# Layer 1's memory attention at the start of the layer instead of at its end

## The chip, the cores and the metric

The kernel runs on one core of one Trainium2 chip, and the metric is the device time of one execution in microseconds. The engines meant below are PE (the matrix engine; PEld is its loading of weights), ACT (the scalar engine), DVE (the vector engine), POOL, and SP, which here issues the loads of the weights. Each engine works through its own instructions in a fixed order. PSUM is the small memory that PE writes its results to, in banks of 128 x 512 fp32.

## The reference, cut to what matters

One inference step of a decoder of two layers runs over 256 prompt tokens and 8 decode sequences of one token, 264 columns in all, with 2048 features. Layer 0 mixes tokens by windowed attention, layer 1 by a gated linear recurrence (HGRN2) with 12 heads of 128. Each layer has besides 4 memory heads, which attend to 256 memory rows: for the prompt these are projected from `mem_prompt`, for each decode sequence they come from a cache of its own. The 12 recurrence heads and the 4 memory heads make 16 blocks of 128 features, which are gated and projected:

```
mq, g, q, f, iv = split(h @ w_in)
fg = lb + (1 - lb) * sigmoid(f)                 # decay, per head and token
state[t] = fg[t] * state[t-1] + (1 - fg[t]) outer iv[t]
o = silu(q)[t] @ state[t];  o = o * rsqrt(mean(o*o) + eps) * norm_w
mem = softmax(mq @ mk.T / sqrt(128)) @ mv       # mk, mv: projected, or cached
y = concat(o, mem) * silu(g) @ w_out
h = layer_norm(alpha * h + y) * ln_w + ln_b
```

## The kernel before, in words

All activations lie transposed, features on the 128 partitions and the 264 columns along the row. The weights come as tiles of 128 x 2048 fp32 (1 MB), one for each block of 128 output features. A class `Stream` (from L50) takes them in one fixed list of *units*: SP loads a tile into one of 4 raw buffers (L77), ACT rounds it to fp16 into one of 4 split buffers (`hl`, L92), DVE takes the remainder (L93), and then the unit's function runs. A projection (`proj`) is 48 matmuls of 264 columns: 16 blocks of the contraction, each in three passes, weights' high half by the data's high half (L297), by its low half (L298), and weights' low half by the data's high half (L299). It goes to one of two PSUM banks ("pj"), from which the next engine reads it. Cache tiles and recurrence states come through the same stream; a cache tile is used by 64 matmuls of one or two columns (mss, L646/L647, for key scores; mso, L690/L691, for sums of values), a state tile (half as large) by 17 (hos).

Longer work that hangs on several units is written as *side* generators: `hg_side(pi)` for a pair of heads of the recurrence, `memp_side` for the prompt's memory attention, the layer norm. After each unit `pump(1)` advances them by a step, and `drain()` finishes them. `hg_side` goes through the levels 1 to 64 of a tree over the prompt's blocks (products hs on PE, then copies and products on DVE and ACT), then builds the head outputs (hpo, L1079 to L1081), reads them to `osb` (ACT L1083), squares them (L1087), sums the squares over partitions by a matmul (rms, L1092), takes the reciprocal root by a Ln (L1093) and an Exp (L1095) on ACT, each with a load of its function table (ACT_TABLE_LOAD) before it, and scales (DVE L1098). For heads 8 to 11 the result is multiplied by the gate later, in `gate_by`: DVE L722, ACT L723 (the fp16 high half, in `bhl`), DVE L724 (the low half). The 16 output projections (`out_unit`) contract over these 16 blocks in order, c = 0 to 15, so that block c = 10 and 11 of every output need heads 10 and 11.

The order of layer 1's units before: memory keys and values; for each pair of heads f, f, v, v, then q, state and (heads 0 to 7) gate g of each head; then the four memory queries mq, the prompt's four memory sides tied to the last of them; then key cache tiles ck0 to ck3 and value cache tiles cv0 to cv3 with the late gates g8 to g13 behind the first six of them, and g14, g15 at the end; then the outputs. The compiler's scheduler takes the program in this order and fixes, from its own timing model, the order of the instructions on each engine; it may place a unit's small pieces in the midst of another's matmuls. Names in the rows below: g113 is gate 13 of layer 1, o10 and o11 are its outputs 0 and 1, hl151 is the split tile of unit 151 of the stream; hpo5, rms50 and rms51 belong to the last pair, heads 10 and 11. PSUM tags are pj (2 banks), pt (2), pv (1), ms (1) and sc (2).

Of the kernel before, what the change touches and what calls it, by code (L numbers as in the profile page):

```python
# [129 lines left out]
def trunk_kernel(  # L130
# [37 lines left out]

    def bank(tag, bufs, name):
        return ps.tile([P, 512], F32, tag=tag, name=name, bufs=bufs)  # L170

    stream = Stream(nc, cp, 4, 4)

# [379 lines left out]
        nc.scalar.activation(mix[:, :NQ, TP:T], pov, AF.Copy, scale=1.0 / (SA * SP))  # L553
        done[0].add("swa")

    def mq_unit(h):
        def fn(hl):
            pt = proj(hl, xhl, T, f"mq{h}")
            split_from(mqhl[:, 0, h], mqhl[:, 1, h], pt, 1.0 / SW)

        return fn
# [72 lines left out]
    def ck_unit(l, t):  # L634
        def fn(hl):
            v = hl.rearrange("p s (b h m) -> p s b h m", b=2, h=NM)
            if t == 0:
                mst["s"] = bank("ms", 1, f"mss{l}")
            sv = mst["s"][:, :128].rearrange("p (m r s) -> p m r s", m=2, s=2)
            for bb in range(2):  # L640
                b = 2 * t + bb
                for h in range(NM):
                    for m in range(2):
                        r = b * NM + h
                        ms = slice(m * P, (m + 1) * P)
                        mm(sv[:, m, r], v[:, 0, bb, h, ms], mqhl[:, :, h, TP + b], start=True, stop=False)  # L646
                        mm(sv[:, m, r, 0:1], v[:, 1, bb, h, ms], mqhl[:, 0, h, TP + b : TP + b + 1], start=False, stop=True)  # L647
            if t == 3:
                mems_soft(l)

        return fn
# [24 lines left out]
    def cv_unit(l, t):  # L676
        def fn(hl):
            v = hl.rearrange("p s (b m f) -> p s b m f", b=2, m=2)
            R = TS * NM
            phl = mst["p"].rearrange("p (m r) s -> p m r s", m=2)  # L680
            if t == 0:
                mst["o"] = bank("ms", 1, f"mso{l}")
            ov = mst["o"][:, :64].rearrange("p (h b s) -> p h b s", h=NM, s=2)
            for bb in range(2):
                b = 2 * t + bb
                for h in range(NM):
                    r = b * NM + h
                    f = slice(h * P, (h + 1) * P)
                    for m in range(2):
                        mm(ov[:, h, b], v[:, 0, bb, m, f], phl[:, m, r], start=m == 0, stop=False)  # L690
                        mm(ov[:, h, b, 0:1], v[:, 1, bb, m, f], phl[:, m, r, 0:1], start=False, stop=m == 1)  # L691
            if t == 3:
                so = cp.tile([P, NM, TS], F32, tag="mso", name=f"msos{l}")
                nc.vector.tensor_reduce(so, ov, axis=AX.X, op=ALU.add)
                nc.scalar.activation(mix[:, NQ:, TP:T], so, AF.Copy, scale=1.0 / (SA * SP))
                done[l].add("mem")

        return fn
# [174 lines left out]
        stream.add(wb(w_mk[1], h), mk_unit(1, h))  # L873
    for t in range(4):
        stream.add(wb(w_mv[1], t), mv_unit(1, t))

    l1 = ExitStack()
    H = {}
# [13 lines left out]
    def f_unit(h):  # L892
        def fn(hl):
            if h == 0:
                drain()
                open_l1()
            p1 = H["p"]
            pt = proj(hl, xhl, T, f"f{h}")
            i = h % 2
            if i == 0:  # L900
                cur["fg"] = p1.tile([P, 2, T], F32, tag="fg", name=f"fg{h}", bufs=2)
                cur["kk"] = p1.tile([P, 2, T], F32, tag="kk", name=f"kk{h}", bufs=2)
                cur["ks8"] = p1.tile([P, 2, TS], F32, tag="ks8", name=f"ks8{h}", bufs=2)
            fg, kk, ks8 = cur["fg"][:, i], cur["kk"][:, i], cur["ks8"][:, i]
            th = p1.tile([P, T], F32, tag="th", name=f"th{h}", bufs=2)
            nc.scalar.activation(th, pt, AF.Tanh, scale=0.5 * CP)
            half, mid, half_k, nhalf_k = (hl_lb[:, k, h : h + 1] for k in range(4))
            nc.scalar.activation(fg, th, AF.Identity, bias=mid, scale=half)
            nc.scalar.activation(kk, th, AF.Identity, bias=half_k, scale=nhalf_k)
            nc.vector.tensor_scalar_mul(ks8, kk[:, TP:T], 1.0 / (SA * SK))  # L910

        return fn
# [193 lines left out]
    def state_unit(h):  # L1106
        def fn(hl):
            p1 = H["p"]
            pi, i = h // 2, h % 2
            raw = stream.raw[state_at[h]][:, : TS * P]  # L1110
            R = raw.rearrange("p (b v) -> p b v", b=TS)
            v = hl[:, :, : TS * P].rearrange("p s (b v) -> p s b v", b=TS)
            vr, fgs, ks8 = cur["vr"][:, i], cur["fg"][:, i, TP:T], cur["ks8"][:, i]
            qs, ks, vts = (cur[n][:, i, TP:T] for n in ("q", "kk", "vt"))
            if i == 0:
                osb[pi] = p1.tile([P, 2, T], F32, tag="osb", name=f"osb{pi}", bufs=2)
            qk = p1.tile([P, TS], F32, tag="qk", name=f"qk{h}", bufs=2)
            qf = p1.tile([P, TS], F32, tag="qf", name=f"qf{h}", bufs=2)
            qfh = p1.tile([P, TS, 2], F16, tag="qfh", name=f"qfh{h}", bufs=2)
            nc.vector.scalar_tensor_tensor(qf, qs, SA * 0.5 * CP, fgs, op0=ALU.mult, op1=ALU.mult)  # L1120
            nc.vector.scalar_tensor_tensor(qk, qs, P * 0.5 * CP / SK, ks, op0=ALU.mult, op1=ALU.mult)
            nc.scalar.activation(qfh[:, :, 0], qf, AF.Copy)
            nc.vector.tensor_tensor(qfh[:, :, 1], qf, qfh[:, :, 0], op=ALU.subtract)
            po = bank("ms", 1, f"hos{h}")
            pov = po[:, : 2 * TS].rearrange("p (b s) -> p b s", s=2)
            for b in range(TS):
                mm(pov[:, b], v[:, 0, b], qfh[:, b], start=True, stop=False)
                mm(pov[:, b, 0:1], v[:, 1, b], qfh[:, b, 0:1], start=False, stop=True)
            pq = po[:, 2 * TS : 3 * TS]
            mm(pq, ones_rms, qk, start=True, stop=True)  # L1130
            nc.vector.tensor_reduce(qf, pov, axis=AX.X, op=ALU.add)
            nc.vector.tensor_tensor(qk, pq, vts, op=ALU.mult)
            nc.vector.scalar_tensor_tensor(osb[pi][:, i, TP:T], qf, 1.0 / (SA * SA), qk, op0=ALU.mult, op1=ALU.add)
            for g in range(2):
                pvb = bank("pt", 2, f"vb{h}{g}")
                for bb in range(4):
                    mm(pvb[:, bb * P : (bb + 1) * P], H["sel"][:, 4 * g + bb], vr, start=True, stop=True)
                for bb in range(4):
                    b = 4 * g + bb
                    s = R[:, b]  # L1140
                    nc.scalar.activation(s, s, AF.Copy, scale=fgs[:, b : b + 1])
                    nc.vector.scalar_tensor_tensor(
                        s, pvb[:, bb * P : (bb + 1) * P], ks8[:, b : b + 1], s, op0=ALU.mult, op1=ALU.add
                    )
            nc.gpsimd.dma_start(ss_o[pi, :, i * TS * P : (i + 1) * TS * P], raw)
# [4 lines left out]
    for pi in range(HD // 2):  # L1150
        for part, unit in (("f", f_unit), ("v", hv_unit)):
            for i in range(2):
                stream.add(wb(w_in1, NB1[part] + 2 * pi + i), unit(2 * pi + i))
        for h in (2 * pi, 2 * pi + 1):
            stream.add(wb(w_in1, NB1["q"] + h), hq_unit(h))
            state_at[h] = len(stream.units)
            stream.add(state[pi][:, (h % 2) * TS * P : (h % 2 + 1) * TS * P], state_unit(h), SA, whole=True)
            if h < NG1:
                stream.add(wb(w_in1, NB1["g"] + h), early_gate(h))
    for h in range(NM):  # L1160
        stream.add(wb(w_in1, NB1["mq"] + h), mq_unit(h))

    def mem1_sides(fn):
        return with_side(fn, [lambda h=h: memp_side(1, h) for h in range(NM)])

    u = stream.units[-1]
    stream.units[-1] = (u[0], mem1_sides(u[1]), *u[2:])

    def g1(j):
        stream.add(wb(w_in1, NB1["g"] + j), gate_unit(1, j))  # L1170

    late = deque(range(NG1, NC))
    for n, (c, unit, t) in enumerate([(c_mk, ck_unit, t) for t in range(4)] + [(c_mv, cv_unit, t) for t in range(4)]):
        stream.add(c[1, t], unit(1, t), SA)
        if late and (late[0] < NQ or n == 7 or late[0] < NQ + 2 and n > 3):
            g1(late.popleft())
    while late:
        g1(late.popleft())
    for i in range(NC):
        stream.add(wb(w_o[1], i), out_unit(1, i))  # L1180

    def after(i):
# [5 lines left out]
        if 1 <= i < 3:  # L1188
            spread_bias(2 * i - 2)
            spread_bias(2 * i - 1)  # L1190
        pump(1)
        for rows in due:
            rows()
        due[:], later[:] = later, []
# [141 lines left out]
```

## Time and profile before

| what | value |
|---|---|
| median of 3 runs | 912.54 us (911.29 to 913.2) |
| the profiled execution | 912.57 us, span 910.8 us |
| busy: PE, PEld, DVE, ACT, POOL | 895.5, 760.7, 701.9, 577.0, 34.6 us |
| mean granted clock of PE | 0.995 |
| from HBM | 179.80 MB read, 216 GB/s over the span with what is written |

The span runs from the first to the last instruction; the time of the execution holds a little more around it. Busy time of PE is the sum over its matmuls. In a table by stretches of time, the columns are the stretch, its length, the busy time of PE, PEld, DVE, ACT and POOL (with the number of instructions), then the granted clock of PE as a share of full speed, the busy share of the DMA engines and GB/s.

### The profile page before, as it was taken

Reading aid. Unit: us, or ns where it says so; the run is one execution under the profiler, and the core shown is the slowest. Engines: PE = TensorE matmul, PEld = TensorE weight load, DVE = VectorE, ACT = ScalarE, POOL = GpSimd, SP = SyncE. Lnnn points to the kernel's source line nnn. Section 1 sums busy time; section 2 is a strip of 40 time slices with the busy share of each in tenths; the row PEclk is TensorE's granted clock in tenths of the full one; section 3 lists DMA queues with packets and bytes.
Section 4 is the critical chain, followed back from the end, with each engine's and each line's share of the span. In section 5 each row is a group of like instructions: output and inputs, shape, how many; then the busy total and the mean of one; then the engine's idle time right before and its main releaser. Section 6 shows DMA issues by size and latency. Waiting matters only on the chain.

```text
span 910.8 us, 21139 instructions
## 1 busy us (share of the span) xinstructions
PE 895.5 (98%) x8913; PEld 760.7 (84%) x8913; DVE 701.9 (77%) x1280; ACT 577.0 (63%) x980; POOL 34.6 (4%) x63
## 2 busy tenths in 40 slices
PE   9999999999999999999999999999999999899996
PEld 6888989678888888866888888888888888788885
DVE  6869877669886666696697897978789899767645
ACT  6757776567664543576766777676778676945323
POOL 1100010000000000002000000000000000000000
PEclk9999999999999999999999999999999999999998
DMA  9999566567685555555384555727454778566302
GB/s 345 383 335 330 189 244 217 194 210 259 257 320 189 204 208 187 191 203 195 127 308 146 196 183 185 282 100 268 150 212 165 264 270 318 186 226 230 141 1 96
DMA packets 36412, 198.41 MB, mean 218 GB/s; under 512 B 4572, under 2 KB 8445, under 8 KB 16093
## 3 DMA queue, kind: packets, MB, share of 16 engines
q1 hardware_dynamic: 31632, 181.55, 55.6%
q0 software_dynamic: 4640, 15.44, 4.6%
q8 instruction: 70, 1.15, 0.5%
q14 instruction: 26, 0.21, 0.1%
q10 hardware_dynamic: 44, 0.07, 0.0%
HBM read 179.80 MB, written 17.22 MB: 216 GB/s over the span
## 4 chain that ended last, share of the span: by engine, by line
PE 87%; ACT 5%; DVE 5%; DMA 2%; issue 1%; SPq 0%; ACTq 0%; DVEq 0%
PE o L297 6%; PE o L299 6%; PE o L298 6%; PE g L299 6%; PE g L297 6%; PE g L298 6%; PE q L297 2%; PE hv L298 2%; PE hv L297 2%; PE q L298 2%; PE q L299 2%; PE hv L299 2%; ACT hl L92 2%; PE f L299 2%; PE f L297 2%; PE f L298 2%
## 5 line engine op out<-in xcount | busy, mean ns | idle before, releaser
L93 DVE SCALAR_TENSOR_TENSOR hl<-raw,hl 128x2048 f16<-128x2048 f32 (+2 forms) x176 | 376.9, 2145 | 96.6 <-ACT hl L92 95.9
L92 ACT ACTIVATE hl<-raw 128x2048 f16<-128x2048 f32 (+2 forms) x176 | 314.2, 1790 | 118.1 <-PE o L299 73.9
L297 PEld LDWEIGHTS <-hl 128*128 128x128 f16 (+1 forms) x2176 | 209.9, 98 | 34.0 <-issue 2.9
L299 PEld LDWEIGHTS <-hl 128*128 128x128 f16 (+1 forms) x2176 | 209.9, 98 | 33.4 <-DVE hl L93 2.1
L298 PEld LDWEIGHTS <-hl 128*128 128x128 f16 (+1 forms) x2176 | 209.9, 98 | 32.1 <-issue 1.6
L299 PE MATMUL g<-xhl,hl 128*128 128x264 f16 x512 | 141.3, 276 | 1.5 <-DVE hl L93 1.5
L297 PE MATMUL g<-xhl,hl 128*128 128x264 f16 x512 | 141.5, 276 | 0.0
L298 PE MATMUL g<-xhl,hl 128*128 128x264 f16 x512 | 141.3, 276 | 0.0
L299 PE MATMUL o<-mix,hl 128*128 128x264 f16 x512 | 141.2, 276 | 0.0
L298 PE MATMUL o<-mix,hl 128*128 128x264 f16 x512 | 141.2, 276 | 0.0
L297 PE MATMUL o<-mix,hl 128*128 128x264 f16 x512 | 140.8, 276 | 0.3 <-DVE xres L742 0.3
L297 PE MATMUL q<-xhl,hl 128*128 128x264 f16 x192 | 53.0, 276 | 1.0 <-DVE kst L245 1.0
L297 PE MATMUL f<-xhl,hl 128*128 128x264 f16 x192 | 52.9, 276 | 0.4 <-DVE mvhl L245 0.4
L297 PE MATMUL hq<-xhl,hl 128*128 128x264 f16 x192 | 53.0, 276 | 0.0
L298 PE MATMUL hq<-xhl,hl 128*128 128x264 f16 x192 | 53.0, 276 | 0.0
L299 PE MATMUL hq<-xhl,hl 128*128 128x264 f16 x192 | 53.0, 276 | 0.0
L298 PE MATMUL hv<-xhl,hl 128*128 128x264 f16 x192 | 53.0, 276 | 0.0
L297 PE MATMUL hv<-xhl,hl 128*128 128x264 f16 x192 | 53.0, 276 | 0.0
L299 PE MATMUL hv<-xhl,hl 128*128 128x264 f16 x192 | 53.0, 276 | 0.0
L298 PE MATMUL q<-xhl,hl 128*128 128x264 f16 x192 | 53.0, 276 | 0.0
L299 PE MATMUL q<-xhl,hl 128*128 128x264 f16 x192 | 53.0, 276 | 0.0
L299 PE MATMUL f<-xhl,hl 128*128 128x264 f16 x192 | 52.9, 276 | 0.0
(311 smaller groups left out, 1625.4 us busy)
## 6 DMA issues: line engine op xcount, KB each, us to landing
raw<-in_w_in SPq DMA_DIRECT2D x88, 1024.0 KB, 5.8
raw<-in_w_o SPq DMA_DIRECT2D x32, 1024.0 KB, 4.9
raw<-in_w_mk SPq DMA_DIRECT2D x8, 1024.0 KB, 4.8
raw<-in_w_mv SPq DMA_DIRECT2D x8, 1024.0 KB, 5.1
raw<-in_c_mk SPq DMA_DIRECT2D x8, 1024.0 KB, 5.2
raw<-in_c_mv SPq DMA_DIRECT2D x8, 1024.0 KB, 4.9
raw<-in_state SPq DMA_DIRECT2D x12, 512.0 KB, 5.0
out_ss<-raw POOLq DMA_DIRECT2D x12, 512.0 KB, 2.9
```

Of the source, the lines that this page charges most:

```text
L92: hi = self.nc.scalar.activation(hl[:, 0, s], raw[:, s], AF.Copy, scale=scale)
L93: lo = self.nc.vector.scalar_tensor_tensor(hl[:, 1, s], raw[:, s], scale, hl[:, 0, s], op0=ALU.mult, op1=ALU.subtract)
L297: mm(out, lhs(0), rhs(0), start=start, stop=False)
L298: mm(out, lhs(0), rhs(1), start=False, stop=False)
L299: return mm(out, lhs(1), rhs(0), start=False, stop=stop)
```

## The change

The four memory queries of layer 1 and the prompt's memory sides now come right after the layer's memory keys and values, ahead of f0; what finishes the sides of layer 0 (`drain`) moves from f0 to the first query. The four key cache tiles come behind f0, f1, v0 and v1, value cache tiles cv0 and cv1 behind the states of heads 0 and 1, cv2 and cv3 behind f2 and f3. The late gates come in the order 12, 13, 14, 15, 8, 9, 10, 11, with two steps of the sides behind each. Key scores, value sums and the state units' sums hos, which each took the one "ms" bank in turn, now share a single bank of the layer, each a part of 128 columns. Line numbers after the first hunk grow by 7 to 13. No arithmetic is added or left out.

```diff
+    msb = {}
+
+    def sums(l, part):
+        if l not in msb:
+            msb[l] = bank("ms", 1, f"sums{l}")
+        return msb[l][:, 128 * part : 128 * part + 128]
...
-    def mq_unit(h):
+    def mq_unit(h, fresh=False):
         def fn(hl):
+            if fresh:
+                drain()
...
-                mst["s"] = bank("ms", 1, f"mss{l}")
+                mst["s"] = sums(l, 0)
...
-                mst["o"] = bank("ms", 1, f"mso{l}")
+                mst["o"] = sums(l, 1)
...
+    for h in range(NM):
+        fn = mq_unit(h, h == 0)
+        if h == NM - 1:
+            fn = with_side(fn, [lambda h=h: memp_side(1, h) for h in range(NM)])
+        stream.add(wb(w_in1, NB1["mq"] + h), fn)
...
-            po = bank("ms", 1, f"hos{h}")
+            po = sums(1, 2 + h % 2)
...
                 stream.add(wb(w_in1, NB1[part] + 2 * pi + i), unit(2 * pi + i))
+                if pi == 0:
+                    t = 2 * (part == "v") + i
+                    stream.add(c_mk[1, t], ck_unit(1, t), SA)
+                elif pi == 1 and part == "f":
+                    stream.add(c_mv[1, 2 + i], cv_unit(1, 2 + i), SA)
...
+            if h < 2:
+                stream.add(c_mv[1, h], cv_unit(1, h), SA)
             if h < NG1:
                 stream.add(wb(w_in1, NB1["g"] + h), early_gate(h))
...
-    late = deque(range(NG1, NC))
-    for n, (c, unit, t) in enumerate([(c_mk, ck_unit, t) for t in range(4)] + [(c_mv, cv_unit, t) for t in range(4)]):
-        stream.add(c[1, t], unit(1, t), SA)
-        if late and (late[0] < NQ or n == 7 or late[0] < NQ + 2 and n > 3):
-            g1(late.popleft())
-    while late:
-        g1(late.popleft())
+    late_units = range(len(stream.units), len(stream.units) + NC - NG1)
+    for j in (*range(NQ, NC), *range(NG1, NQ)):
+        stream.add(wb(w_in1, NB1["g"] + j), gate_unit(1, j))
...
-        pump(1)
+        pump(2 if i in late_units else 1)
```

First place, on PE, where the last pair of heads is normed. Before, the two sums of squares stand in the middle of gate 13's projection (hl151):

```order
L299 MATMUL g113_11094<-xhl_93,hl151_10905 128x264
L297 LDWEIGHTS hl151_10905
L297 MATMUL g113_11094<-xhl_93,hl151_10905 128x264
L298 LDWEIGHTS hl151_10905
L298 MATMUL g113_11094<-xhl_93,hl151_10905 128x264
L1092 MATMUL rms50_10818<-osq50_10758,ones_rms_81 128x264
L299 LDWEIGHTS hl151_10905
L299 MATMUL g113_11094<-xhl_93,hl151_10905 128x264
L1092 MATMUL rms51_10821<-osq51_10760,ones_rms_81 128x264
L297 LDWEIGHTS hl151_10905
```

Now, at the same work of the same pair (hl156 and hl157 are the tiles of the outputs o10 and o11, and `mix_95` is the row of gated blocks):

```order
L306 MATMUL o11_11469<-mix_95,hl157_11278 128x264
L1094 MATMUL hpo5_11196<-qa5_10781,s15_11190 128x128
L1092 MATMUL hpo5_11196<-st5_10780,vn10_10278 128x128
L1093 MATMUL hpo5_11196<-st5_10780,vn10_10278 128x128
L1094 MATMUL hpo5_11196<-qa5_10781,s15_11190 128x128
L1105 MATMUL rms50_11268<-osq50_11204,ones_rms_81 128x264
L1105 MATMUL rms51_11271<-osq51_11206,ones_rms_81 128x264
L304 LDWEIGHTS hl156_11208
L304 MATMUL o10_11411<-mix_95,hl156_11208 128x264
L304 LDWEIGHTS hl157_11278
L304 MATMUL o11_11469<-mix_95,hl157_11278 128x264
```

The last pair's outputs and sums of squares moved from gates 12 and 13 to the first two outputs. Ahead of them stand 30 matmuls of o10 and 30 of o11 (blocks 0 to 9), and the two rows behind them, of o10 and of o11, are those of block 10.

Second place, on ACT, the same pair, now (osb5 is the copy of hpo5, osq its squares, sil110 and sil111 the gates of heads 10 and 11):

```order
L1096 ACTIVATE osb5_10491<-hpo5_11196 128x2x256
L1100 ACTIVATE osq50_11204<-osb5_10491 128x264
L1100 ACTIVATE osq51_11206<-osb5_10491 128x264
L1106 ACT_TABLE_LOAD
L1106 ACTIVATE osq50_11204<-rms50_11268,eps_rms_83 128x264
L1106 ACTIVATE osq51_11206<-rms51_11271,eps_rms_83 128x264
L1108 ACT_TABLE_LOAD
L1108 ACTIVATE osq50_11204<-osq50_11204 128x264
L1108 ACTIVATE osq51_11206<-osq51_11206 128x264
L732 ACTIVATE mix_95<-sil110_11332 128x264
L732 ACTIVATE mix_95<-sil111_11392 128x264
```

What moved: the same instructions stood before in the time of gates 12 and 13, with other gates' work between the last Exp and the rows of heads 10 and 11; now nothing stands between.

Third place, on ACT, the splits around the gate of head 1 (g11). Before (hl88 is the state of head 1, hl89 the tile of g11, hl90 and hl91 are the two after it, of f2 and f3):

```order
L92 ACTIVATE hl88_5961<-raw88_5721 128x1024
L953 ACTIVATE vn0_5829<-hvp1_5954 128x256
L1122 ACTIVATE qfh0_5967<-qf0_5966 128x8
L1141 ACTIVATE raw88_5721<-raw88_5721,fg0_5710 128x128 x8
L92 ACTIVATE hl89_6026<-raw89_6020 128x2048
L727 ACTIVATE mix_95<-g10_6029 128x264
L92 ACTIVATE hl90_6080<-raw90_6022 128x2048
```

Now (hl97 is the state of head 1, hl98 the cache tile cv1, hl99 the tile of g11, hl100 that of f2):

```order
L92 ACTIVATE hl97_6550<-raw97_6542 128x1024
L736 ACTIVATE mix_95<-g10_6588 128x264
L250 ACTIVATE msphl1_6419<-mback1_6416 128x64
L966 ACTIVATE vn0_6212<-hvp1_6422 128x256
L92 ACTIVATE hl98_6585<-raw98_6544 128x2048
L1154 ACTIVATE raw97_6542<-raw97_6542,fg0_5950 128x128 x8
L92 ACTIVATE hl99_6639<-raw99_6546 128x2048
L736 ACTIVATE hqs0_6481<-hq1_6642 128x264
L92 ACTIVATE hl100_6719<-raw100_6548 128x2048
```

Between the state's split and g11's there is now the split of a cache tile. The buffer that g11's split takes is the one of cv0, and it comes free with cv0's last matmul; between that and g11's first, PE has 16 matmuls of the projection of head 1's q and 8 of the 16-row matmuls vb (L1150, before L1137).

8 lines of the change are left out of this document (removed).

## The prediction

> **What bounds the kernel now.** I read the page's first part and the chain, then windows of 20 us around the place that the change empties, then windows of 1 us there.
>
> ```profile
> PE 895.5 (98%) x8913; PEld 760.7 (84%) x8913; DVE 701.9 (77%) x1280; ACT 577.0 (63%) x980; POOL 34.6 (4%) x63
> PE 87%; ACT 5%; DVE 5%; DMA 2%; issue 1%; SPq 0%; ACTq 0%; DVEq 0%
> ```
>
> PE is busy for 98% of the span and makes 87% of the chain: only an idle PE, or a PE at a lower clock, can be gained or lost. The change issues the same matmuls, so what has to be found is where PE stands still before and where it will stand still after.
>
> ```profile
> core 0: us, PE busy (x) PEld busy (x) DVE busy (x) ACT busy (x) POOL busy (x), PEclk, DMA share, GB/s
> 460.00:480.00 20.00, 20.00 (x213) 17.56 (x212) 18.58 (x37) 11.82 (x17) 0.54 (x1) 1.00 0.90 332
> ...
> 780.00:800.00 20.00, 17.24 (x240) 14.83 (x238) 18.28 (x30) 18.02 (x32) 0.00 (x0) 0.91 0.60 224
> 800.00:820.00 20.00, 19.70 (x177) 17.18 (x176) 12.77 (x23) 9.01 (x15) 0.00 (x0) 1.00 0.55 195
> 820.00:840.00 20.00, 20.00 (x181) 17.39 (x179) 15.24 (x17) 10.44 (x12) 0.00 (x0) 1.00 0.63 216
> ```
>
> In the recurrence (460 to 480) and in the outputs (820 to 840) PE is full; in 780 to 800, where the last value cache tiles stand before, it loses 2.76 us and its clock falls to 0.91. The last row also gives the price of a projection: 181 matmuls in 20.00 us are 0.1105 us each, 48 of them 5.3 us.
>
> ```profile
> 784.00:785.00 1.00, 0.83 (x33) 0.74 (x30) 0.49 (x3) 1.00 (x1) 0.00 (x0) 1.00 0.00 0
> 785.00:786.00 1.00, 0.18 (x1) 0.11 (x2) 0.66 (x1) 1.00 (x4) 0.00 (x0) 1.00 0.03 8
> 786.00:787.00 1.00, 0.73 (x5) 0.58 (x5) 1.00 (x1) 1.00 (x6) 0.00 (x0) 0.77 0.00 0
> 787.00:788.00 1.00, 1.00 (x7) 0.69 (x6) 1.00 (x3) 1.00 (x3) 0.00 (x0) 0.50 0.00 0
> 788.00:789.00 1.00, 1.00 (x19) 0.82 (x18) 1.00 (x5) 1.00 (x2) 0.00 (x0) 0.50 0.49 74
> 789.00:790.00 1.00, 1.00 (x25) 0.87 (x23) 1.00 (x4) 1.00 (x2) 0.00 (x0) 0.53 0.62 213
> 790.00:791.00 1.00, 0.97 (x9) 0.73 (x7) 1.00 (x3) 1.00 (x2) 0.00 (x0) 1.00 0.95 401
> 791.00:792.00 1.00, 0.00 (x0) 0.00 (x0) 1.00 (x1) 1.00 (x2) 0.00 (x0) 1.00 0.87 360
> 792.00:793.00 1.00, 0.52 (x5) 0.47 (x6) 1.00 (x4) 1.00 (x2) 0.00 (x0) 1.00 0.00 0
> ```
>
> Two stalls are seen, 1.26 us in 784 to 787 and 1.51 us in 790 to 793, with ACT and DVE full through both. After the first the clock is at half for about 3.4 us (786.8 to 789.6 by the shares 0.77, 0.50, 0.50, 0.53: 1.70 us of clock lost). The second, longer one did not lower it.
>
> **What is removed.** The cache tiles leave this place, and with them both stalls: 2.76 us. The lost clock is worth at most its 1.70 us; most of the matmuls in it are projections and scores whose rate goes with the clock, so I take all. The 0.30 us of 800 to 820 belongs to an output and stays. Sum: −4.5 us (bounds −2.8 and −4.8).
>
> **The tail that it builds.** The last pair's hg_side had 20 units behind its last state before (4 mq, 8 cache tiles, 8 gates); now it has 8 gates, and the order on PE puts its outputs hpo and its sums of squares behind 30 matmuls each of o10 and o11. Blocks 10 and 11 of these two outputs need that pair; both "pj" banks are theirs, so o12 cannot start; the layer's other PE work is done. PE must wait for a chain on ACT and DVE. What this chain takes is in the trace, where it ran hidden, read on PE, ACT and DVE:
>
> ```profile
> 772.55 0.39 PE L1081 MATMUL hpo<-qa,s 128*128 128x128 f32 x2
> 776.27 0.61 PE L1092 MATMUL rms<-osq,ones_rms 128*128 128x264 f32 x2
> ```
>
> ```profile
> 773.39 0.57 ACT L1083 ACTIVATE osb<-hpo 128x512 f32<-128x512 f32 x1
> 773.99 0.74 ACT L1087 ACTIVATE osq<-osb 128x264 f32<-128x264 f32 x2
> 774.63 1.89 ACT L92 ACTIVATE hl<-raw 128x2048 f16<-128x2048 f32 x1
> ...
> 776.70 0.23 ACT L243 ACTIVATE msphl<-mback 128x64 f16<-128x64 f32 x1
> 776.95 1.28 ACT L1093 ACT_TABLE_LOAD   x1
> 778.25 0.85 ACT L1093 ACTIVATE osq<-rms,eps_rms 128x264 f32<-128x264 f32 x2
> 779.12 1.28 ACT L1095 ACT_TABLE_LOAD   x1
> 780.41 0.74 ACT L1095 ACTIVATE osq<-osq 128x264 f32<-128x264 f32 x2
> 782.15 0.42 ACT L723 ACTIVATE mix<-sil 128x264 f16<-128x264 f32 x1 [1.00 <-DVE sil L722]
> ```
>
> ```profile
> 776.56 2.29 DVE L93 SCALAR_TENSOR_TENSOR hl<-raw,hl 128x2048 f16<-128x2048 f32 x1 [2.52 <-ACT hl L92]
> ...
> 780.87 0.90 DVE L1098 SCALAR_TENSOR_TENSOR mix<-osb,small_t,osq 128x264 f32<-128x264 f32 x2 [1.54 <-ACT osq L1095]
> 781.68 0.43 DVE L722 SCALAR_TENSOR_TENSOR sil<-sil,mix 128x264 f32<-128x264 f32 x1
> ```
>
> Set 0 at the end of hpo. With 0.1 us for the hand-over (an estimate; rows such as 781.68 to 782.15 leave 0.04 after 0.43 of work): osb to 0.7 (0.60 start to start), the squares to 1.4 (0.74), the first table load to 2.7 (1.28), two Ln to 3.6 (0.87), the second load to 4.9 (1.29), the first scaling starts at 5.35 (780.41 to 780.87), the multiplication by the gate 0.81 later (780.87 to 781.68) at 6.15, the high half 0.47 later (to 782.15) at 6.6, and it ends at 7.05. Then block 10 of o10 can start; its low half is a DVE instruction on as many elements as L722, another 0.43, while two or three matmuls of high halves run: 0.2 us more. Of these 7.25 us PE works some 0.6 on the two rms. **PE idle: 6.6 us.** No split lies in this chain, as the order on ACT shows; if one did, 1.9 us would come on top. Below 4.9 it can hardly be: ACT's own work in the chain (0.57, 0.74, 1.28, 0.85, 1.28, 0.37, 0.42) is 5.5, less the 0.6 of rms.
>
> Such a stall can cost clock as well. Before, 1.26 us of idle time among small matmuls brought 1.70 us of loss, 1.51 us at once brought none. A stall of over 5 us is nearer to the first, but half speed may pass in part while PE stands: bounds 0 and 1.7, I take 1.2.
>
> The Trainium skill ("TensorE: Matmul & The Clock Gate", "Part 1: The HAM clock gate") has a free-running window of about 3.4 us, and an idle window puts the clock to half until a busy one has passed. The trace's 3.4 us at half agrees in length, and its undisturbed 1.51 us does not contradict; by the page alone the new stall would be followed by up to 1.7 us of loss, an estimate that lies inside the bounds above.
>
> **The front.** Eight cache tiles come between projections, where PE was full. On PE each takes little; on ACT and DVE each costs as much as a projection's tile.
>
> ```profile
> 461.04 0.61 PE L1137 MATMUL vb<-vr,sel_t 16*128 16x128 f16 x8
> ...
> 739.03 0.17 PE L646 MATMUL mss<-mqhl,hl 128*128 128x2 f16 x1
> 739.32 0.16 PE L647 MATMUL mss<-mqhl,hl 128*128 128x1 f16 x1
> L299 PE MATMUL g<-xhl,hl 128*128 128x264 f16 x512 | 141.3, 276 | 1.5 <-DVE hl L93 1.5
> ```
>
> Twelve cache matmuls start within 0.29 us, so 64 take about 1.7 us, against 1.89 of ACT and then 2.29 of DVE for the tile's split. The last row is the second stall above, all of it a gate that waited for its low half after two cache tiles in a row. The same arises at g11: its split takes cv0's buffer, so it starts after cv0's last matmul and is done 4.2 us later; PE has 16 matmuls of hq1 (1.8 us), vb (0.6 us) and two passes of g11 (0.2 us) to cover it. **Stall: 1.6 us**, with DVE at 18.58 of 20 us in such a stretch even without cache tiles. The same walk through the orders, from the last mq to f3, leaves all tiles before g11 covered, and gives 0.7 us at f3 (its low half; two of the four raw buffers are held by states that wait to be written out) and 0.1 where cv1 waits for DVE to read hos1, since these sums now share its PSUM bank; cv0's like wait lies behind g10. Front: **+2.4 us**, with 0 as lower bound (walk too pessimistic by a split) and 6.4 as upper (all four value tiles cost what cv0 does).
>
> The moved mq and prompt sides cost nothing of their own: layer 0 has this order before, and the key tiles stand between projections whose 5.3 us cover 4.2. The 16 additional pump steps issue no instruction.
>
> **Sum** against the profiled execution of 912.57 us, which is the median of the runs within 0.03: 912.6 − 4.5 + 6.6 + 1.2 + 2.4 = **918.3 us**, 0.6% slower.
>
> **Rivals.**
>
> *Tail stall alone.* Clock kept, front covered: 912.6 − 4.5 + 6.6 = 914.7; with the removal at its bound of 4.8, 914.4. For it: 1.51 us of idle time did not cost clock, and a hand-made walk can err by 2 us in the front. Against: g11's cover is short by more than half. Chance 0.15.
>
> *Front bound by DVE.* A split that is late makes the next one late: 912.6 − 4.5 + 6.6 + 1.7 + 6.4 = 922.8. For it: DVE at 18.58 of 20. Against: over the whole front ten projections and eight cache tiles give PE 67 us, DVE's 18 full splits 41. Chance 0.14.
>
> *Faster.* The chain of the last pair is hidden after all: the gain of 4.5 us stays, and the place where this is decided is o10: if hpo were done before block 9 of o10 and o11, by at least 7 us, PE would not stop. Then 912.6 − 4.5 + up to 2.4 = 908.1 to 910.5. For it: before, the chain was hidden at the same cost. Against: the order on PE is fixed, with hpo behind 60 of the 60 matmuls that could hide the chain. Chance 0.03.
>
> *Table loads that drain.* If each load first emptied ACT for as long as it takes itself, the tail would grow by 2 x 1.28, to 920.9. Against: in the rows the load starts 0.02 us after the instruction ahead (776.93 to 776.95) and the Ln 0.02 after the load. Chance 0.03. The Trainium skill ("ScalarE: Activation LUTs", "What ACT_TABLE_LOAD costs") gives 1283 ns for the load, which the trace shows, and some 1380 ns of drain, which it does not; by the page the sum would be about 921.1, an estimate.
>
> **Chances.** The forecast has 0.65, with a range of its own of 916 to 920.5. The range for 8 in 10 takes in most of the tail-alone case and of the DVE case: **914.2 to 922**. A difference of 0.2%, 1.8 us, is about what runs of this kernel tell from none. Faster: 0.03 and a little for the unforeseen, 0.05. Within 0.2% (to 914.4): half of the tail-alone case, 0.08. Slower: 0.87.
>
> **What would show it.** Right: idle time of about 6 us on PE ahead of o10's block 10, ended by ACT's L732, with the clock near half for some us behind it; the 1.5 us of a gate that waits for L93 now at g11, in the first third of layer 1; no loss in the former place between gates. Wrong: a full PE over o10 and o11; a stall at each cache tile; or idle time ahead of f0, where the prompt's memory sides now stand.

## The result, and the profile after

| what | before | changed |
|---|---|---|
| median of the runs | 912.87 us (911.29 to 913.66, 4 runs) | 923.26 us (922.21 to 925.0, 4 runs) |
| profiled execution, span | 912.57, 910.8 us | 923.42, 921.6 us |
| PE busy, mean clock | 895.5 us, 0.995 | 897.8 us, 0.995 |

The change makes the kernel slower by 1.1%: ratio 1.011, 95% interval 1.0091 to 1.0129, where 918.3 us with a range of 914.2 to 922 was forecast. The direction holds, the size does not. Of all the runs below, a single one counts as slow (value tiles late, 1321.96 us at a clock of 0.65), and it enters no figure here.

The changed kernel's waits of PE (what waited, what ended the wait; us in all, times, longest):

```profile
PE o L304 <- ACT mix L732: 4.8, 1, 4.8
PE hs L304 <- ACT qsp L1000: 2.7, 2, 2.5
PE g L306 <- DVE hl L93: 1.6, 1, 1.6
...
PE rms L1105 <- ACT osq L1100: 1.1, 1, 1.1
PE hd L1043 <- DVE hqs L737: 1.1, 1, 1.1
```

And its windows of 20 us in layer 1 (columns as before):

```profile
480.00:500.00 20.00, 18.37 (x199) 15.13 (x198) 14.33 (x32) 12.91 (x23) 0.54 (x1) 1.00 0.55 195
500.00:520.00 20.00, 18.20 (x269) 15.85 (x268) 19.10 (x31) 12.80 (x17) 0.54 (x1) 1.00 0.93 336
520.00:540.00 20.00, 19.16 (x203) 17.03 (x203) 17.08 (x30) 15.23 (x32) 0.00 (x0) 1.00 0.66 235
540.00:560.00 20.00, 18.99 (x186) 15.62 (x184) 13.10 (x36) 17.51 (x31) 1.08 (x2) 1.00 0.50 179
...
780.00:800.00 20.00, 19.69 (x211) 17.06 (x210) 19.93 (x36) 11.32 (x19) 0.00 (x0) 1.00 0.52 191
800.00:820.00 20.00, 16.83 (x161) 14.69 (x159) 8.80 (x15) 10.54 (x16) 0.54 (x1) 0.99 0.47 165
820.00:840.00 20.00, 17.24 (x137) 14.26 (x137) 12.09 (x17) 10.68 (x14) 0.00 (x0) 0.84 0.32 109
```

The old stalls among the last gates are gone. In their place stand a large one at the first outputs (5.93 us idle in 800 to 840, and a clock of 0.84) and three in the front, at 495 us (1.63 us, g11), 518 us (2.52 us, across the edge of two windows) and 559 us (1.14 us). From 480 to 560 PE is idle for 5.28 us; before, it was full there, but for 0.17 us. The first two of these four windows in the kernel before:

```profile
480.00:500.00 20.00, 20.00 (x222) 17.62 (x221) 14.74 (x33) 13.92 (x33) 0.00 (x0) 1.00 0.35 120
500.00:520.00 20.00, 20.00 (x190) 17.28 (x189) 16.04 (x45) 15.69 (x29) 1.08 (x2) 1.00 0.54 206
```

To sum it, take from the trace the start of every matmul to the start of the next, less the lower quartile of that spacing for its shape in the kernel before; this counts idle time and low clock alike.

| PE time lost, us | before | changed | difference |
|---|---|---|---|
| up to the last mv of layer 1 | 9.7 | 9.7 | 0.0 |
| front: from there to 60 us ahead of the last gate | 8.6 | 14.9 | +6.3 |
| the last 60 us of gates | 5.3 | 1.9 | −3.3 |
| outputs | 0.8 | 8.7 | +7.8 |

The differences add up to +10.8 us, as the two spans do (921.6 − 910.8).

The tail, on ACT in the changed kernel, from the outputs of the last pair of heads to its gated blocks:

```profile
815.71 0.60 ACT L1096 ACTIVATE osb<-hpo 128x512 f32<-128x512 f32 x1 [2.87 <-PE hpo L1094]
816.34 0.74 ACT L1100 ACTIVATE osq<-osb 128x264 f32<-128x264 f32 x2
817.10 1.28 ACT L1106 ACT_TABLE_LOAD   x1
818.39 0.85 ACT L1106 ACTIVATE osq<-rms,eps_rms 128x264 f32<-128x264 f32 x2
819.26 1.28 ACT L1108 ACT_TABLE_LOAD   x1
820.55 0.73 ACT L1108 ACTIVATE osq<-osq 128x264 f32<-128x264 f32 x2
822.28 0.77 ACT L732 ACTIVATE mix<-sil 128x264 f16<-128x264 f32 x2 [1.00 <-DVE sil L731]
```

From 815.71 to the end of the first L732 (822.28 + 0.42) are 6.99 us: it is the chain that the prediction took from the hidden one, step for step. The clock, in windows of 1 us:

```profile
819.00:820.00 1.00, 0.00 (x0) 0.00 (x0) 0.00 (x0) 0.98 (x2) 0.00 (x0) 0.86 0.00 0
...
822.00:823.00 1.00, 0.24 (x2) 0.17 (x2) 0.85 (x3) 0.71 (x2) 0.00 (x0) 0.50 0.00 0
823.00:824.00 1.00, 1.00 (x6) 0.64 (x5) 0.52 (x2) 0.05 (x1) 0.00 (x0) 0.50 0.00 0
...
826.00:827.00 1.00, 1.00 (x9) 0.76 (x7) 0.00 (x0) 0.00 (x0) 0.00 (x0) 0.72 0.00 0
```

It fell to half at 819.7, while PE stood still, and stayed there until 826.6: 6.8 us, of which PE worked 3.8 at half speed, some 1.9 us lost.

Two of the front's stalls the prediction did not have. The first, at 518 us, on ACT:

```profile
515.26 1.91 ACT L92 ACTIVATE hl<-raw 128x2048 f16<-128x2048 f32 x1 [0.18 <-DMA raw<-in_w_in]
518.58 1.91 ACT L92 ACTIVATE hl<-raw 128x2048 f16<-128x2048 f32 x1 [1.41 <-DMA raw<-in_w_in]
520.39 0.40 ACT L1000 ACTIVATE qsp<-qa 128x256 f16<-128x256 f32 x1
```

PE waits for the short copy at 520.39, which feeds the hs products. On ACT it stands behind the split of a tile for which PE has no need yet, and that split waited 1.41 us for its load. The second, at 559 us:

```profile
551.48 1.28 ACT L1106 ACT_TABLE_LOAD   x1
552.78 0.48 ACT L1106 ACTIVATE osq<-rms,eps_rms 128x264 f32<-128x264 f32 x1
553.28 1.28 ACT L1108 ACT_TABLE_LOAD   x1
554.57 0.42 ACT L1108 ACTIVATE osq<-osq 128x264 f32<-128x264 f32 x1
555.01 1.28 ACT L1106 ACT_TABLE_LOAD   x1
...
556.80 1.28 ACT L1108 ACT_TABLE_LOAD   x1
558.10 0.42 ACT L1108 ACTIVATE osq<-osq 128x264 f32<-128x264 f32 x1
558.43 0.37 ACT L736 ACTIVATE hqs<-hq 128x264 f32<-128x264 f32 x1
```

In the first pair of heads the order is now Ln, Exp, Ln, Exp, with four table loads where there were two: 2.6 us more on ACT, and the silu of q (L736), for which the next pair's hd waits, comes behind it; its second half, on DVE, then stands behind the norm's own scalings and runs at 559.65. The program writes Ln, Ln, Exp, Exp; the scheduler chose the other order. The kernel before has 12 such loads in the six pairs, the changed one 14.

### The profile page after: what moved, and what is told of

It reads as the page before. It is cut to its first block, busy times and chain, and to the rows that moved or that the text cites. A ratio compares the mean times of both kernels' runs of the same rounds, so it can differ in the third digit from the quotient of the medians.

```text
span 921.6 us, 21135 instructions
## 1 busy us (share of the span) xinstructions
PE 897.8 (97%) x8913; PEld 760.7 (83%) x8913; DVE 701.0 (76%) x1280; ACT 580.0 (63%) x982; POOL 34.5 (4%) x63
## 3 DMA queue, kind: packets, MB, share of 16 engines
q8 instruction: 70, 1.15, 0.5%
## 4 chain that ended last, share of the span: by engine, by line
PE 90%; ACT 5%; DVE 3%; DMA 2%; issue 0%; ACTq 0%; DVEq 0%
PE o L304 6%; PE o L305 6%; PE o L306 6%; PE g L304 6%; PE g L306 5%; PE g L305 5%; PE q L304 2%; PE hv L304 2%; PE hv L306 2%; PE q L305 2%; PE q L306 2%; PE hv L305 2%; PE hq L304 2%; PE hq L305 2%; PE hq L306 2%; PE f L306 2%
## 5 line engine op out<-in xcount | busy, mean ns | idle before, releaser
L93 DVE SCALAR_TENSOR_TENSOR hl<-raw,hl 128x2048 f16<-128x2048 f32 (+2 forms) x176 | 376.7, 2143 | 89.7 <-ACT hl L92 89.2
L92 ACT ACTIVATE hl<-raw 128x2048 f16<-128x2048 f32 (+2 forms) x176 | 314.5, 1790 | 130.8 <-PE o L306 76.6
```

Of the source, the lines that this page charges most:

```text
L92: hi = self.nc.scalar.activation(hl[:, 0, s], raw[:, s], AF.Copy, scale=scale)
L93: lo = self.nc.vector.scalar_tensor_tensor(hl[:, 1, s], raw[:, s], scale, hl[:, 0, s], op0=ALU.mult, op1=ALU.subtract)
```

## The experiments

The theory: the work that was moved had been the cover of the last pair's chain, and without it the outputs wait; value cache tiles next to states stall the front. Ratios are to the kernel before, run on the same chip; its median there was 914.2 us for the runs e and f, 914.0 for g and 913.4 for h.

**Two more banks for the outputs.**

```diff
-    def proj(hl, src, n, name):
+    def proj(hl, src, n, name, tag="pj"):
...
-        pt = bank("pj", 2, name)
+        pt = bank(tag, 2, name)
...
-            pt = proj(hl, bhl, T, f"o{l}{i}")
+            pt = proj(hl, bhl, T, f"o{l}{i}", "pt" if l == 1 and i in (2, 3) else "pj")
```

> The changed kernel, with the third and the fourth output of layer 1 sent to the two pt banks of PSUM, which are free by then, so that PE has 60 more matmuls (6.7 us) to run while heads 10 and 11 are normed; nothing else is different. Theory (the last pair of heads lost its cover): the idle time of 6.2 us ahead of block 10 goes to under 1 us and the half clock behind it with it, 923.3 - 6.2 - 1.7 = 915.4, between 914.5 and 917. Rival (the outputs are as much bound by the splits on ACT and DVE, so that PE waits later instead): 919 or more. The front of layer 1 stays as it is under both.

Measured: 921.03 us, ratio 1.0077 (1.0056 to 1.0097). The tail shrank only to 2.7 + 0.3 us of waiting with a half clock behind it. The time lost in the outputs, counted as in the table, went from 8.7 to 5.2 us; in this execution the front lost 2.4 more than the changed kernel's, at half clock. What is left of the tail is on PE and ACT:

```profile
821.06 0.48 ACT L1106 ACTIVATE osq<-rms,eps_rms 128x264 f32<-128x264 f32 x1 [1.15 <-PE rms L1105]
821.56 1.28 ACT L1108 ACT_TABLE_LOAD   x1
822.85 0.42 ACT L1108 ACTIVATE osq<-osq 128x264 f32<-128x264 f32 x1
823.29 1.28 ACT L1106 ACT_TABLE_LOAD   x1
```

The time lies where the rival had it, but not for the rival's reason: the cover works, and the chain behind it grew. The two sums of squares now stand behind 34 more matmuls of the outputs and start 3.2 us after hpo ends (817.2 to 820.4; in the changed kernel 1.1), so the first Ln waits 1.15 us for them, and this order has four loads in the last pair.

**Half of the move.** The kernel before, with the four mq units and the prompt's sides placed ahead of f0 as in the change, and the old loop of cache tiles and gates left in place.

```diff
+    for h in range(NM):
+        fn = mq_unit(h, h == 0)
+        if h == NM - 1:
+            fn = with_side(fn, [lambda h=h: memp_side(1, h) for h in range(NM)])
+        stream.add(wb(w_in1, NB1["mq"] + h), fn)
...
-    for h in range(NM):
-        stream.add(wb(w_in1, NB1["mq"] + h), mq_unit(h))
```

> The kernel before, with only the four memory queries and the prompt's memory sides moved to the start of layer 1; the eight cache tiles and the gates stay at the end, in the old order, and PSUM is as before. Theory (the cache tiles are what stalls the front, and late work is what covers the last pair): no stall at g11 and none ahead of the outputs; the two stalls at the last cache tiles stay in some form: 910 to 914. Rival (the queries and the prompt's sides were the cover that counted): a stall of 3 us or more ahead of or in the outputs, 916 or more. Rival (queries at the start delay the recurrence): 916 or more with idle time before the first recurrence head.

Measured: 928.97 us, ratio 1.0165 (1.0141 to 1.0189), the first rival. Its waits of PE begin

```profile
PE o L297 <- ACT mix L725: 4.9, 1, 4.9
PE g L299 <- DVE hl L93: 2.8, 3, 1.1
PE o L298 <- DVE mix L726: 2.0, 1, 2.0
```

With the four queries and the prompt's sides away, the outputs wait for gated blocks even though all cache tiles still stand in the last stretch. That queries and sides were cover is borne out. What part of the 6.9 us is their absence and what the order (the last pair has four table loads here too) is not shown. The trace has, besides, 3.4 us of waits at 789 to 792 and 20.5 us at half clock after 790, which no run prices.

**Value tiles late.** The changed kernel, with

```diff
-                elif pi == 1 and part == "f":
-                    stream.add(c_mv[1, 2 + i], cv_unit(1, 2 + i), SA)
...
-            if h < 2:
-                stream.add(c_mv[1, h], cv_unit(1, h), SA)
...
-    for j in (*range(NQ, NC), *range(NG1, NQ)):
+    for j in range(NG1, NC):
+        if j < NQ:
+            stream.add(c_mv[1, j - NG1], cv_unit(1, j - NG1), SA)
         stream.add(wb(w_in1, NB1["g"] + j), gate_unit(1, j))
...
-        pump(2 if i in late_units else 1)
+        pump(2 if i >= late_from else 1)
```

where `late_from` is the first unit of the second pair. Each value tile stands ahead of its gate.

> The changed kernel, with the four value cache tiles put one each behind late gates 8 to 11, the late gates in their old order 8 to 15, and two steps of the sides after every unit from the second pair of heads on. Theory: without value tiles the front has no stall at g11 nor at the hs products behind them, and the four tiles cover the last pair, whose sums of squares come out 0.7 of a projection ahead of the first output: 912.9 less the 4.5 of the old stalls, 908 to 911. Rival (value tiles stall wherever they stand, since a split costs 4.2 us against 1.7 on PE): four stalls of about 1 us among the gates, 913 to 917.

Measured: 922.81 us, ratio 1.0099 (1.0074 to 1.0124). The tail is gone and so is g11's stall, as the theory had it, but the gain was eaten:

```profile
PE hs L304 <- ACT qsp L1000: 5.0, 3, 2.1
PE hd L1043 <- DVE hqs L737: 3.9, 2, 2.0
```

This order has 18 table loads, six more than before; the two waits of hd and the first of the late hs waits (at 761.7) follow the alternation in three pairs. The longest hs wait, at 765.9, is a copy behind the split of a value tile (cv2, 765.68), so the value tiles have a part in it; how large, this run does not show. Both expectations missed.

**Five raw buffers.** `Stream(nc, cp, 4, 4)` becomes `Stream(nc, cp, 5, 4)`.

> The changed kernel with five raw buffers for loads instead of four. It tells why the hs products behind cv1 waited 2.65 us: ACT's copy for them stands behind the split of a tile whose load landed late. Theory (late because two of the four raw buffers are held by states until these are written out): the stall goes to under 0.7 us, 923.3 - 2 to 2.6 = 920.5 to 921.5, the tail stays. Rival (late because the DMA engines are full there, share 0.95 to 1.06 from 515 to 521 us): the stall stays over 2 us, 922.5 to 924.

Measured: 922.17 us, ratio 1.0099 (1.0076 to 1.0121). The wait of 2.5 us went, as the theory had it:

```profile
PE f L304 <- DVE mix L737: 1.0, 1, 1.0
PE hs L304 <- ACT qsp L1000: 0.9, 3, 0.5
```

So the load was late because the raw buffers were held, not because the DMA engines were full. Of the 2 us, one came back as a wait of f, and the time missed the theory's 920.5 to 921.5; its interval overlaps the changed kernel's, so a gain in time is not shown.

**No dependence.** In layer 1's outputs, `src[:, s, c]` becomes `src[:, s, k]` with k = c − 2 for c in (10, 11): blocks 8 and 9 are contracted twice, and 10 and 11 are left out of the outputs; all matmuls (8913) are there.

> The changed kernel, whose layer 1 outputs contract blocks 8 and 9 twice and leave blocks 10 and 11 out, so that nothing in the outputs waits for the last pair of heads; all its work is still done, and the number of matmuls is the same. It prices the tail. Theory (the last pair without cover): no idle time and no half clock at the first outputs, 923.3 - 6.2 - 1.7 = 915.4, between 914 and 917. Rival (the outputs' front is held by something else as well, splits or loads): over 918.

Measured: 916.23 us, ratio 1.0026 (1.0011 to 1.0041). No wait of an output is left, and the time lost in the outputs is 0.4 us. Against the changed kernel's 1.011 the tail is worth 0.84%, 7.7 us (some 2 us either way by the two intervals); the theory had 7.9.

**One Exp for a pair.**

```diff
+        osq = p1.tile([P, 2, T], F32, tag="osq", name=f"osq{pi}", bufs=1)
...
-            sq = p1.tile([P, T], F32, tag="osq", name=f"osq{pi}{i}", bufs=2)
+            sq = osq[:, i]
...
+        nc.scalar.activation(osq, osq, AF.Exp, scale=-0.5)
...
-            nc.scalar.activation(sq, sq, AF.Exp, scale=-0.5)
```

> The changed kernel, with one Exp over both heads of a pair instead of one for each, so that the order on ACT can no longer be Ln, Exp, Ln, Exp with four table loads; the order then holds two loads a pair. Theory (the alternation in the first pair held up ACT by 2.6 us, and hd behind it by 1.3): the stall of hd at 558 us goes, 923.3 - 1.3 = 922.0, between 921 and 922.8; table loads in the rms lines 12 instead of 14. Rival (ACT has slack there, and the wait was for DVE's own queue): unchanged, 923.3 within 0.7.

Measured: 924.67 us, ratio 1.0115 (1.0091 to 1.0138). The wait of hd is gone from the list, and ACT now reads

```profile
555.05 1.28 ACT L1107 ACT_TABLE_LOAD   x1
556.35 0.85 ACT L1107 ACTIVATE osq<-rms,eps_rms 128x264 f32<-128x264 f32 x2
557.22 1.28 ACT L1108 ACT_TABLE_LOAD   x1
558.51 0.64 ACT L1108 ACTIVATE osq<-osq 128x528 f32<-128x528 f32 x1
```

That alone does not show the cause, since PE comes to this place later here: it ran at half clock twice on the way (498.9 to 502.4 and 522.8 to 526.3). The next run settles it. That the theory's 1.3 us come off the time is not shown; the profiled execution (926.31) is the slowest of six, 923.29 the fastest, and the half clock in the front, of which more below, is what it lost instead.

**Banks and one Exp together.**

> The changed kernel with both: the third and fourth output in the pt banks, and one Exp a pair. Theory (what was left of the tail with the pt banks, 3.1 us of idle time and a half clock, came from four table loads in the last pair instead of two): the chain is 7 us again and hidden behind 56 matmuls and more, tail under 0.5 us; with the first pair's 1.3: 921.0 - 3.1 - 1.7 - 1.3 = 914.9, between 914 and 917. Rival (the last pair is late for another reason): over 918, with idle time of over 2 us ahead of block 10.

Measured: 917.35 us, ratio 1.0034 (1.0018 to 1.005). Against the banks alone (921.03) one Exp is worth 3.7 us here: the tail is down to 1.3 us of waiting and no half clock. In what is left the first Ln again waits 1.15 us for the sums of squares, which PE runs behind 34 matmuls of the outputs. In the front both traces have two stretches at half clock; with the banks alone hd waits 1.14 us at 560, with one Exp it does not wait. So the alternation is the cause of that stall.

**The kernel before, alternating.**

```diff
-            a = cp.tile([P, T], F32, tag="sil", name=f"sil{l}{j}", bufs=3)
+            a = cp.tile([P, T], F32, tag="sil", name=f"sil{l}{j}", bufs=4)
...
-            if len(fin[l]) >= 3:
+            if len(fin[l]) >= 3 + l:
...
-        if late and (late[0] < NQ or n == 7 or late[0] < NQ + 2 and n > 3):
+        if late:
```

> The kernel before, with a fourth buffer for gates that wait for their blocks, so that every cache tile at the end, the last two value tiles too, has a gate behind it (ck0 g8 ck1 g9 ... cv3 g15); nothing moves to the front. It tells what the stalls that the change removes were worth, and whether they can be had at the end. Theory (two value tiles in a row made both stalls and the low clock): 2 to 4.5 us faster than before, ratio 0.995 to 0.998. Rival (ACT and DVE are full at the end in any order, and gates 12 to 15 now wait for the prompt's memory sides, which reach into the first outputs): the same or slower, ratio 0.999 or more.

Measured: 911.50 us, ratio 0.9968 (0.9955 to 0.998), faster than before. In 780 to 800 PE is idle for 0.80 us instead of 2.76:

```profile
780.00:800.00 20.00, 19.20 (x246) 15.91 (x245) 19.11 (x32) 17.27 (x30) 0.00 (x0) 0.83 0.63 235
```

The clock is at half there for 6.8 us instead of 3.4, so this one execution shows less of the gain than the median does.

The stalls that the change was rid of could be had, in part, where they stood, by a gate between the last two value tiles.

**Alternating, with the two banks.** The two diffs together.

> The kernel before with every cache tile at the end followed by a gate, as in the run that alternates them, and with the third and fourth output of layer 1 in the pt banks. It looks for a version that beats both kernels. Theory (in the alternating kernel the outputs lose 1.6 us, waiting for a block that is gated late and for a pj bank that is read late; two banks more let PE go on): 1 to 1.6 us less than the alternating kernel's ratio of 0.9968, ratio 0.995 to 0.996. Rival (the banks are still in use by the prompt's memory sides, which reach into the first outputs): no gain or a loss, ratio 0.9965 or more.

Measured: 910.12 us, ratio 0.9958 (0.9941 to 0.9974), the fastest kernel found; no wait of an output is left. It beats the kernel before by 0.4% and the changed one by 1.5%.

**Value tiles late, no dependence.** The value tiles and gates as in the run with value tiles late, `pump` as in the change, outputs as in the run without dependence.

> The changed kernel without the dependence (its outputs contract blocks 8 and 9 twice and leave blocks 10 and 11 out), and with the four value cache tiles put one each behind late gates 8 to 11 instead of into the front, late gates in the order 8 to 15. Against the run without the dependence alone it prices the value tiles in the front. Theory (value tiles behind states cost g11's 1.6, the hs products' 2.6 and some half clock): ratio to before 0.996 to 1.000, 3 to 6 us under the run with the dependence alone (1.0026). Rival (the queries and key tiles at the start slow the recurrence all the same, or value tiles stall among the gates): ratio 1.002 or more.

Measured: 912.13 us, ratio 0.9978 (0.996 to 0.9997). The front is whole again:

```profile
480.00:500.00 20.00, 20.00 (x189) 16.36 (x188) 15.49 (x37) 10.99 (x22) 0.54 (x1) 1.00 0.58 193
500.00:520.00 20.00, 20.00 (x229) 17.65 (x227) 17.10 (x35) 16.22 (x31) 0.54 (x1) 1.00 0.74 287
```

Counted as in the table, the front loses 8.6 us, as before the change: the four key tiles and the queries at the start cost nothing there. Value tiles in the front instead of among the late gates cost 1.0026 − 0.9978 = 0.48%, 4.4 us (some 2 either way), together with the table loads that their order brought.

This run shows something else of the loads. Its last pair comes after the load that the program itself places for the layer norm (`preload_act_table_set("natural_log_exp_and_others")`, L757, at 814.13), and runs Ln and Exp in turns without any load:

```profile
819.10 0.48 ACT L1107 ACTIVATE osq<-rms,eps_rms 128x264 f32<-128x264 f32 x1 [0.20 <-PE rms L1106]
819.62 0.42 ACT L1109 ACTIVATE osq<-osq 128x264 f32<-128x264 f32 x1
```

The second Ln (819.95) and Exp (820.44) follow in the same way. One table holds both functions, then, and the load between Ln and Exp is not forced. Placing that load ahead of each pair was not run, nor is it shown whether the gates' silu would then need one of its own.

**A bank of its own for the states' sums.** `po = sums(1, 2 + h % 2)` becomes `po = bank("pt", 2, f"hos{h}")`.

> The changed kernel with the state units' sums in a pt bank of PSUM instead of the bank they share with the key scores and value sums. Theory (sharing costs nothing that shows, since no wait on PE names the reader of these sums): the stalls at g11 and ahead of the outputs stay as they are, 921 to 925, ratio 1.009 to 1.013. Rival (the shared bank chains value tiles to the states and so makes the front late): g11 and hs stalls go, 919 or less, ratio 1.006 or less.

Measured: 928.37 us, ratio 1.0151 (1.0119 to 1.0182): slower than with the shared bank, outside both expectations. The wait of 4.8 us at the outputs is unchanged and g's waits for L93 still sum to 1.7. That the shared bank costs time which an own one would save is refuted. The stalls themselves do not tell, since the order differs in many places: the wait of hs at 518 is gone, another of 1.5 us stands at 580. In this execution the front is at half clock from 493.7 to 503.9, 10.2 us; why is open. The sums now take turns with vb and pk in the two pt banks.

**The move, mended.** Value tiles late with two steps of the sides, one Exp, two banks.

> The changed kernel with the full contraction, mended at the three places found: value tiles behind late gates 8 to 11 and two steps of the sides after every unit from the second pair of heads on, one Exp a pair, third and fourth output in the pt banks. It asks whether the move can pay at all. Theory (the front is as without value tiles, ratio 0.9978; the last pair's sums of squares stand 35 matmuls, 3.9 us, ahead of the first block that needs them, and the chain behind them takes 5 to 6): a stall of 1 to 2 us with a half clock, ratio 0.999 to 1.003. Rival (with the steps taken twice as fast the hs products wait again for ACT, as in the run with the value tiles late): ratio 1.005 or more.

Measured: 920.10 us, ratio 1.0071 (1.0059 to 1.0083), the rival. The wait of the outputs is down to 0.3 us, and table loads are 12, but

```profile
PE g L306 <- DVE hl L93: 3.2, 2, 1.9
```

The hs products wait three times for ACT's copy of qsp, 2.2 us in all. Before the longest wait, one of g, DVE runs 2.75 us of state updates and copies (774.20 to 776.95) between the two halves of a gate's split: the steps taken twice as fast bring small work into the queues ahead of the splits. The parts that work alone do not add up; that this is because each edit gives the whole layer another order is argued, not shown.

## Why the prediction was wrong in size

*What is removed* (−4.5, bounds −2.8 to −4.8): the two stalls went. By the spacing of the matmuls the late gates gained 3.3 us, inside the bounds and 1.2 short of the value taken. The step at fault took the whole lost clock of 1.70 us as time: among the matmuls at half clock are 31 of one or two columns, 0.027 us apart, against 0.025 at full clock; they take 0.9 of the 3.4 us, so some 0.4 us was no loss. The new wait of hs at 781 takes another 0.3; the remaining 0.5 is open. (The shares put that half clock at 786.5 to 789.9, not 786.8 to 789.6; the sum of 1.70 is right.)

*The tail* (6.6 idle, 1.2 clock, 7.8 in sum): right in its mechanism. The trace has 4.8 + 1.1 = 5.9 us of idle time and some 1.9 lost to half clock; the loss in the outputs grew by 7.8, and the run without the dependence prices it at 7.7. That the sum is met to the tenth is luck: the idle time is 0.7 lower, the clock 0.7 higher and above its bound of 1.7. The idle time came out lower mainly because the row of 0.61 us was read as both sums of squares and is one; the two take PE 1.16 us.

*The front* (+2.4, bounds 0 and 6.4): the step that failed. g11's stall was predicted as 1.6 and is 1.6. The rest was predicted as 0.8, "The same walk through the orders … leaves all tiles before g11 covered, and gives 0.7 us at f3", and is 4.7. Two terms were missing from it. The walk priced waits for splits, but not the small copies that stand behind a split in ACT's queue: the hs products' wait of 2.5 us is a late load, passed on through L92 to a copy of 0.40 us (shown with five raw buffers). And it did not count the table loads; the order had two more, in a place that the walk did not reach, at 1.1 us (shown by the two banks with and without one Exp). That the copy stands behind the split, and that the loads alternate, could have been read from the order on ACT. About 1 us of the 4.7 lies in neither stall and is open.

*Rivals.* "Front bound by DVE", 922.8 us, came nearest in time, but for another reason: DVE is not full in three of the four windows from 480 to 560 (14.33, 17.08 and 13.10 of 20 us, against 19.10 in the one from 500), and two of the three stalls come from ACT's order. "Table loads that drain" falls: in the tail the Ln starts 0.01 us after its load (817.10 + 1.28 to 818.39) and the load 0.02 after the square, now with nothing to hide behind. What the Trainium skill ("ScalarE: Activation LUTs", "What ACT_TABLE_LOAD costs") gives as a drain of about 1380 ns besides the load is not seen here; the measured 1.28 us is all there is.

*The range* ended at 922. The sum with the front's upper bound of 6.4 is 922.3; the front came out at 6.3, and the removal 1.2 short of its term, so 923.26 lies above both. The pump steps, which the prediction counts as 16 more, are 8 more (8 units, two steps instead of one); no term hung on them.

## What to carry to other kernels

Work at the end of a stage that looks misplaced may be what covers the latency of the stage's last item: before moving it, take the length of that item's chain (here 7 us of ACT and DVE, at the end of 44 us of levels, from hd at 772.1 to hpo at 815.7) and count what is left for PE to do meanwhile. When a list of units is reordered, read the new order on the engine that serves everyone (ACT here) for two things: what short instruction now stands behind a long one that waits for a load, and how often the function tables alternate. A fusion that makes a bad order impossible (one Exp for two) is safer than the order; a table that holds both functions, as in the last pair of the run with value tiles late and no dependence, would make the alternation harmless.

## What the runs showed of the hardware

The clock goes to half after far less idle time than the 5 us of the tail, and not always. Six kernels have the same stall of 1.63 us at g11; after it the changed kernel and the one with five raw buffers kept their clock, and four others (two banks, no dependence, one Exp, banks and one Exp) did not. Changed, and with two banks:

```profile
490.00:500.00 10.00, 8.37 (x99) 6.47 (x99) 8.55 (x19) 6.03 (x11) 0.54 (x1) 1.00 0.52 177
```

```profile
490.00:500.00 10.00, 8.37 (x87) 5.99 (x86) 8.30 (x20) 5.29 (x8) 0.54 (x1) 0.83 0.63 219
```

The same idle time, 1.63 us, costs no clock in one execution and 1.7 us of it in the other (0.17 of 10 us). Two things can be read from the traces about when.

From the first full clock to the last matmuls, half clock comes in all 14 traces in pieces of 3.4, 6.8 or 10.2 us, multiples of one step of 3.41 us, and the full clock between two pieces lasts such a multiple too: with two banks, 20.48 us from 499.85 to 520.33, six steps. So the clock is set at the edges of a fixed raster. Laid over the stall at g11, the raster of the changed kernel has an edge inside it, and the step that holds the larger part (495.46 to 498.87) has 1.28 us of it; with two banks one step (493.02 to 496.44) has all 1.63, and half clock begins at its end. That cannot be the whole rule: with five raw buffers, too, one step has all 1.63, and the clock stays.

And PE's busy time is not what the clock goes by. In the alternating kernel half clock lasts 6.8 us, from 783.8 to 790.6, and it begins while PE is busy: the step before (780.4 to 783.8) has no idle time, and most of its matmuls have one or two columns. PE first stands still at 783.94:

```profile
783.00:784.00 1.00, 0.94 (x34) 0.85 (x31) 0.58 (x4) 1.00 (x1) 0.00 (x0) 0.89 0.00 0
```

The free-running window of the Trainium skill ("TensorE: Matmul & The Clock Gate", "Part 1: The HAM clock gate") would make it a matter of where in the window a stall falls; the raster of 3.41 us agrees with it, while a half clock after 1.6 us of idle time goes beyond what the page says of a whole idle window. Two executions of such a kernel can therefore differ by 1.7 us for one stall (half of 3.4), and a stall's price needs several runs.
